# One byte offset for every slot of the matmuls' moving operand in a hybrid decoder layer

## The chip, the cores and the metric

The kernel runs on one core of a Trainium2 chip. The metric is the device time of one execution in microseconds (us); the median of three runs of the kernel before is 1404.62 us (1404.37 to 1404.83). A profile of one more execution says where the time goes.

## The reference

One inference step of a one-layer decoder trunk, in fp32, for 256 prompt tokens and 8 sample tokens of width 2048. Cut to the lines that matter:

```python
xn = rms_norm(x, g_mix)
z = xn @ w_in                                  # 2048 x 3584, split among three mixers
y_pool = pool_mixer(u_pool, ...) @ w_pool_br   # 512 -> 2048
y_lru = (h * gelu(u_gel)) @ w_lru_br           # 1024 -> 2048
y_conf = silu(layer_norm(vc, ...)) @ w_conf_br # 512 -> 2048
gates = sigmoid(xn @ w_gate + b_gate)          # 2048 -> 3 x 2048
x = x + (g_a * y_pool + g_b * y_lru + g_c * y_conf) @ w_out
hid = square(relu(rms_norm(x, g_mlp) @ w_up))  # 2048 -> 8192
x = x + hid @ w_down                           # 8192 -> 2048
```

A final RMSNorm follows, and the new states of the three mixers are outputs as well (the array `so_dram`).

## The kernel before

All tokens are worked on together: N = 256 + 8 = 264 columns. Activations lie transposed, 128 channels on the partitions and the 264 tokens along the free axis, so an operand with 2048 channels is 16 slots of 264 fp32 values, 1056 bytes in each partition. A slot is what one matmul streams as its moving operand.

To keep fp32 precision each operand is split into a high part (rounded to the type float32r) and a low part (the rest). One product is three matmuls, `mm3` (L193 to L196): high weights by high activations, high weights by low, low weights by high:

```python
nc.tensor.matmul(ps[:, :N], whi_t, xh, start=first, stop=False)    # L194
nc.tensor.matmul(ps[:, :N], whi_t, xl, start=False, stop=False)    # L195
nc.tensor.matmul(ps[:, :N], wlo_t, xh, start=False, stop=last)     # L196
```

**Operands.** `A` holds 32 slots: 0 to 15 high, 16 to 31 low. It is the operand of w_in, w_gate and w_out, and in the MLP the hidden layer of the first and the third quarter. The MLP's input lies in four tiles of eight slots, named xn2 (`M`, in `bpart`, L722 to L725; the profile writes "xn"), which take over the memory of the tiles `B`: two with the high parts, two with the low parts. The hidden layer of the second and fourth quarter is in `LH` (high) and `Q` (low); the LRU's gates use `L`, the branches `Q` and `LH`. In all of these slots lie one behind the other, 1056 bytes apart.

**Order of the work.** `weight_plan` lists groups, each one product with 512 output columns over up to 2048 input rows, and cuts them into 478 chunks of up to 128 x 1024 weights (two slots, `kt` 0 and 1, by 512 columns). The groups run: w_in (7 groups of 8 chunks; after four chunks of the lru groups the LRU's block weights come between), w_gate with w_pool_br and w_lru_br in four rounds, the last part of w_gate, w_conf_br, w_out, and then four quarters, each w_up (4 groups) and w_down (4 groups). For each slot the program issues four output tiles of three matmuls, twelve in all, before it goes on to the next slot; in the first four chunks (`by_operand`, L903) the same twelve are ordered by operand. The order is written out in Python, instruction by instruction; no scheduler moves it.

**Weights.** SyncE (SP) loads weights into a ring of six slots `raw`: `dma_pair` (L133 to L138) two chunks in one transfer of 1 MB from chunk SINGLE on, `dma_part` (L146) one chunk before. At chunk i the loads of chunks i + 8 and i + 9 are issued. ACT casts a chunk to its high part (`split`, L177) and DVE subtracts to get the low part (L178), three chunks ahead of TensorE (AHEAD = 3), into rings of four (`whi`, `wlo`). Between these casts ACT, DVE and GpSimd (POOL) do the mixers' elementwise work, handed out by costs and credits (`run_bg`).

**States.** The tile `st` collects the new states. At chunk 140 POOL issues its store to `so_dram` (L973).

**Memory.** In the built program the first 16384 bytes of each partition are scratch for transfers that POOL issues, then four constants of 32 bytes each, then the tiles in the order of their lines: raw, whi, wlo, qtmp (later Q), X, A, the four B tiles, L (later LH), G and small ones.

Of the kernel before, what the change touches and what calls it, by code (L numbers as in the profile page):

```python
# [9 lines left out]
F32 = mybir.dt.float32  # L10
F32R = mybir.dt.float32r
AF = mybir.ActivationFunctionType
ALU = mybir.AluOpType
AX = mybir.AxisListType

P = 128
D = 2048
TP = 256
TS = 8
N = TP + TS  # L20
KD = D // P
# [20 lines left out]
O_POOL, O_LC, O_CC, O_H = 1824, 1884, 1908, 2028  # L42
S_OUT = 2036

HEAD = N + 512
FIRST = 8
CH = 1024
# [2 lines left out]
LRU_AT = ((4, 1), (4, 3), (4, 5), (4, 6))  # L50
WARM = 17
LEAD = 4
SINGLE = 18
AHEAD = 3


# [31 lines left out]
def hybrid_step(ctx: ExitStack, tc: tile.TileContext, first, par_in, st_in, wall, y_out, st_out):  # L88
    nc = tc.nc
    cpool = ctx.enter_context(tc.tile_pool(name="cpool", bufs=1))  # L90
# [3 lines left out]
    def f(ap):  # L94
        return ap.bitcast(F32)
# [2 lines left out]
    raw = cpool.tile([P, NRAW, CH], F32, name="raw")  # L98
    whi = cpool.tile([P, NHI, CH], F32R, name="whi")
    wlo = cpool.tile([P, NHI, CH], F32R, name="wlo")  # L100
    qtmp = cpool.tile([P, 16 * N], F32, name="qtmp", tag="Q")
    X = cpool.tile([P, KD, N], F32, name="X")
    A = cpool.tile([P, 32, N], F32R, name="A")
    B = [cpool.tile([P, 8, N], F32, name=f"tmp{i}", tag=f"B{i}") for i in range(4)]
    L = cpool.tile([P, 16, N], F32R, name="L", tag="L")
    G = cpool.tile([P, 24, N], F32, name="G")
    par = cpool.tile([P, NPAR], F32, name="par")
    st = cpool.tile([P, S_OUT], F32, name="st")
# [7 lines left out]
    def pv(name, i=None, n=1):  # L116
        a, b = PCOL[name]
        return par[:, a:b] if i is None else par[:, a + i:a + i + n]

    def acc():  # L120
        return psum.tile([P, 512], F32, name="acc", tag="acc")

    spare = nc.const_aps.tensor(1.0, [P, 2 * P], dtype=mybir.dt.bfloat16)
    Gf = G.rearrange("p a n -> p (a n)")
    pext = qtmp[:, 2900:2900 + 4 * (15 + TP)].rearrange("p (g n) -> p g n", g=4)
    vext = B[3].rearrange("p a n -> p (a n)")[:, 8 * N - 4 * (30 + TP):].rearrange("p (g n) -> p g n", g=4)
    done = set()


# [16 lines left out]
        nc.sync.dma_start(raw[:, c % NRAW, a:b], src[:, a:b])  # L146


    head = [B[i].rearrange("p a n -> p (a n)") for i in (1, 2)]
    gm = head[0]  # L150

    def head_at(k):
# [136 lines left out]
    for c in range(2, 6):  # L289
        dma_x(c)  # L290
        dma_part(c, 0, CH)
    el = B[0].rearrange("p a n -> p (a n)")[:, :8 * (TP + 3)].rearrange("p (a n) -> p a n", a=8)
    nc.gpsimd.memset(el[:, :, 0:3], 0.0)
    nc.gpsimd.memset(vext[:, :, 0:30], 0.0)
    nc.gpsimd.memset(pext[:, :, 0:15], 0.0)
# [3 lines left out]
    def x_of(k):  # L299
        return head_x(k) if k < 4 else X[:, k, :]  # L300

    def x_high(k):
        if k < 2:
            nc.vector.tensor_scalar(A[:, k, :], x_of(k), gm[:, k:k + 1], None, op0=ALU.mult)
        else:
            nc.scalar.activation(A[:, k, :], x_of(k), AF.Copy, scale=gm[:, k:k + 1])

    def x_low(k):
        nc.vector.scalar_tensor_tensor(A[:, 16 + k, :], x_of(k), gm[:, k:k + 1], f(A[:, k, :]),
                                       op0=ALU.mult, op1=ALU.subtract)  # L310

    def x_tile(k):
# [407 lines left out]
    M = []  # L720

    def bpart(k):  # L722
        if not M:
            M.extend(cpool.tile([P, 8, N], F32R, name=f"xn2{i}", tag=f"B{i}") for i in range(4))
        return M[k // 8][:, k % 8, :], M[2 + k // 8][:, k % 8, :]  # L725

    def gate_tile(br, g, m):
        if br == 2:
# [8 lines left out]
    def gate_evac(br, g, m, ps):  # L737
        assert {"b_term", "grp"} <= done and (br != 1 or g % 2 == 0 or "lru" in done) and ("conf" in done or br < 2 or g < 3)
        t = gate_tile(br, g, m)
        nc.vector.tensor_tensor(t, ps[:, :N], rstd, op=ALU.mult)  # L740

        def rest():
            nc.scalar.activation(t, t, AF.Sigmoid, bias=pv("b_gate", br * 16 + g * 4 + m))
            spend(act=0.5)

        spend(dve=0.43)
        later(1 + m // 2, rest)

    def branch_evac(br, g, m, ps):
        assert "grp" in done and (br < 1 or "lru" in done) and (br < 2 or "conf" in done)  # L750
        t = gate_tile(br, g, m)
        k = g * 4 + m
        nc.vector.tensor_tensor(t, ps[:, :N], t, op=ALU.mult)
        spend(dve=0.43)
        if br == 1:
            nc.gpsimd.tensor_tensor(partial(k), t, gate_tile(0, g, m), op=ALU.add)
            spend(pool=0.8)
        if br == 2:
            nc.gpsimd.tensor_tensor(t, t, partial(k), op=ALU.add)
            spend(pool=0.8)  # L760
            later_split(A[:, k, :], A[:, 16 + k, :], t, 1)

    def later_split(hi, lo, x, n):
        def one():
            nc.scalar.copy(hi, x)
            spend(act=0.4)

        def other():
            nc.vector.tensor_tensor(lo, x, f(hi), op=ALU.subtract)
            spend(dve=0.35)  # L770

        later(n, one)
        later(n + 1, other)
# [31 lines left out]

    def hid(q, k):
        if q % 2 == 0:
            return A[:, k, :], A[:, 16 + k, :]
        return LH(k), Q(k)

    def up_evac(q, m, ps):
# [37 lines left out]
    def group(gi):  # L849
        name, k0, _, m = groups[gi]  # L850
        if name == "w_in":
            def rhs(i):
                return A[:, i, :], A[:, 16 + i, :]
            fn = {0: pool_evac, 1: lru_x_copy, 2: lambda c, p: lru_x_evac(4 + c, p), 3: gel_evac,
                  4: lambda c, p: gel_evac(4 + c, p), 5: ca_evac, 6: cb_evac}[m]
            return rhs, fn
        if name == "w_gate":
            return (lambda i: (A[:, i, :], A[:, 16 + i, :])), (lambda c, p: gate_evac(m // 4, m % 4, c, p))
        if name == "w_pool_br":
            assert "grp" in done  # L860
            return (lambda i: (Q(i), Q(8 + i))), (lambda c, p: branch_evac(0, m, c, p))
        if name == "w_lru_br":
            assert "lru" in done
            return (lambda i: (LH(i), LH(8 + i))), (lambda c, p: branch_evac(1, m, c, p))
        if name == "w_conf_br":
            assert "conf" in done
            return (lambda i: (Q(4 + i), Q(12 + i))), (lambda c, p: branch_evac(2, m, c, p))
        if name == "w_out":
            return (lambda i: (A[:, i, :], A[:, 16 + i, :])), (lambda c, p: out_evac(m * 4 + c, p))
        if name == "w_up":  # L870
            return bpart, (lambda c, p: up_evac(m // 4, (m % 4) * 4 + c, p))
        q = k0 // 16
        return (lambda i: hid(q, i)), (lambda c, p: down_evac(q, m * 4 + c, p))
# [52 lines left out]
    for i, ch in enumerate(chunks):  # L926
        now[0] = i
        if i < 5:
            x_tile(2 * i + 6)
            x_tile(2 * i + 7)  # L930
        for half in (0, 1) if i < 2 else (None,):
            split(i + AHEAD, half)
        if i == 12:
            softplus()
            again = first[:, KD:KD + 4 * HEAD].rearrange("p (k c) -> p k c", k=4)[:, :, :N]
            nc.sync.dma_start(X[:, 0:4, :], again)
            nc.vector.tensor_scalar(gfin, pv("g_final"), -0.5, None, op0=ALU.mult)
        if i % 2 == 0:
            dma_pair((i + 8) // 2)
        if i == 2:  # L940
            nc.sync.dma_start(par, par_in)
            nc.sync.dma_start(st[:, :S_IN], st_in)
        kind, gi, c, _ = ch
        if kind == "dense":
            rhs, fn = group(gi)
            n = groups[gi][2] // 2
            if c == 0:
                pss = [acc() for _ in range(4)]
            if i < len(chunks) - 2:
                for kt in range(2):  # L950
                    if i < LEAD:
                        by_operand(i, kt, rhs, pss)
                    for m in range(4 * (i < LEAD), 4):
                        tile_mm(i, c, kt, m, rhs, pss, c == n - 1 and kt == 1)
            elif i == len(chunks) - 1:
                for m in range(4):
                    for b in range(4):
                        tile_mm(i - 1 + b // 2, c - 1 + b // 2, b % 2, m, rhs, pss, b == 3)
            if c == n - 1:
                for m in range(4):  # L960
                    fn(m, pss[m])
                after(gi)
        elif kind == "lru":
            for j in range(2):
                lru_gate_mm(2 * gi + j, i, j)
            if gi == 3:
                lru_tail()
        elif kind == "grp":
            grp_mm(i)
        if i == len(chunks) - 4:  # L970
            nc.scalar.preload_act_table_set(ROOT)
        if i == 140:
            nc.gpsimd.dma_start(st_out, st)  # L973
        if 5 <= i < 9:
            x_squares(i - 5)
        if i == 9:
            later(0, x_sum)
        if i == 12:
            later(0, x_rms)
        run_bg()  # L980
# [9 lines left out]
    for h in range(2):  # L990
        for k, t in enumerate((20, 21 + (KD - 2) % 3, 11)):
            nc.tensor.matmul(ps[h][:, :H2], ones, G[:, t, half[h]], start=k == 0, stop=k == 2)  # L992
    out = [cpool.tile([P, KD, H2], F32, name=f"y{h}", tag=f"B{h}") for h in range(2)]
    last = [acc(), acc()]
    pool_r, tn = G[:, 10, :], G[:, 9, :]
    seed = [rstd[:, half[0]], acc()[:, :H2]]
# [128 lines left out]
```

## Time and profile before

| what | value |
|---|---|
| median of 3 runs | 1404.62 us |
| the profiled execution's own time | 1404.7 us |
| its span, first to last instruction | 1402.9 us |
| granted TensorE clock, mean | 0.998 |
| matmuls | 11421 |
| HBM traffic over the span | 182 GB/s |

The span is what the trace covers; about 1.8 us of the execution's time lie around it. In the profile's rows "PE" is TensorE, "PEld" its weight loads, which overlap the matmuls; matmuls overlap each other, so the duration of one is longer than the distance from one start to the next. A row of the timeline reads: start in us, duration in us, engine, line, operation, output <- inputs, shape. A row of a group ends with the busy time, the mean duration of one in ns, and the idle time before. "SPq" is SyncE's queue.

### The profile page before, as it was taken

To read this page: it belongs to the slowest core of one execution; us is meant where nothing else is said; L and a number is where in the kernel's file an instruction comes from. 1 tells how busy PE (TensorE), PEld (TensorE's weight loads), DVE (VectorE), ACT (ScalarE), POOL (GpSimd) and SP (SyncE) were. 2 spreads that over 40 slices of the span, in tenths; PEclk is the share of its full clock that TensorE was granted. 3 is DMA by queue.
4 is the path that set the end of the run, shared out by engine and by line. 5 is a ranking of instruction groups with operands and counts; after the bars stand their busy time and mean duration, and the time that the engine had idled before them with its cause. 6 is when DMAs were issued, how large, how long until landed. Compare 5 with 4: busy or idle time off the path is not lost.

```text
span 1402.9 us, 26642 instructions
## 1 busy us (share of the span) xinstructions
PE 1392.3 (99%) x11421; PEld 1390.5 (99%) x11421; DVE 835.8 (60%) x1052; ACT 722.3 (51%) x1021; POOL 94.3 (7%) x123
## 2 busy tenths in 40 slices
PE   9999999999999999999999999999999999999997
PEld 9999999999999999999999999999999999999997
DVE  8685787766766658565545444554455544455544
ACT  7757576656664645455544334543344533354544
POOL 0220010110102013010000000000000000000012
PEclk9999999999999999999999999999999999999999
DMA  9555555555655554555555555555555555555551
GB/s 363 170 173 188 185 185 191 181 182 181 210 182 180 179 182 160 202 177 172 192 181 181 180 182 180 181 180 182 179 182 178 183 179 182 181 181 179 180 183 74
DMA packets 39814, 257.49 MB, mean 184 GB/s; under 512 B 4368, under 2 KB 5520, under 8 KB 10896
## 3 DMA queue, kind: packets, MB, share of 16 engines
q1 hardware_dynamic: 39120, 254.15, 53.2%
q8 instruction: 89, 1.46, 0.4%
q0 software_dynamic: 144, 1.04, 0.2%
q10 hardware_dynamic: 432, 0.61, 0.1%
q14 instruction: 29, 0.24, 0.1%
HBM read 252.57 MB, written 3.21 MB: 182 GB/s over the span
## 4 chain that ended last, share of the span: by engine, by line
PE 99%; DVE 0%; DMA 0%; ACT 0%; DVEq 0%; issue 0%
PE acc L196 33%; PE acc L194 33%; PE acc L195 33%; PE acc L903 1%; DMA tmp<-first_dram 0%; DVE y L1014 0%; DVE acc L1005 0%; DVEq L1104 0%; DVE G L1004 0%; DVE acc L1003 0%; PE acc L992 0%; PE acc L271 0%; ACT whi L187 0%; ACT rstd L998 0%; DVE G L834 0%
## 5 line engine op out<-in xcount | busy, mean ns | idle before, releaser
L178 DVE TENSOR_TENSOR wlo<-raw,whi 128x1024 fp32r<-128x1024 f32 (+1 forms) x478 | 584.1, 1224 | 541.8 <-ACT whi L177 541.0
L177 ACT CAST whi<-raw 128x1024 fp32r<-128x1024 f32 (+1 forms) x478 | 495.3, 1039 | 614.2 <-PE acc L195 560.2
L194 PE MATMUL acc<-A,whi 128*128 128x264 f32 x1952 | 556.0, 285 | 0.0
L196 PE MATMUL acc<-A,wlo 128*128 128x264 f32 x1952 | 555.2, 284 | 0.0
L195 PE MATMUL acc<-A,whi 128*128 128x264 f32 x1952 | 554.3, 284 | 0.0
L195 PEld LDWEIGHTS acc<-A,whi 128*128 128x128 f32 x1952 | 368.8, 189 | 0.0
L196 PEld LDWEIGHTS acc<-A,wlo 128*128 128x128 f32 x1952 | 368.1, 189 | 0.0
L194 PEld LDWEIGHTS acc<-A,whi 128*128 128x128 f32 x1952 | 367.9, 188 | 0.0
L194 PE MATMUL acc<-xn,whi 128*128 128x264 f32 x1024 | 291.7, 285 | 0.0
L196 PE MATMUL acc<-xn,wlo 128*128 128x264 f32 x1024 | 291.3, 284 | 0.0
L195 PE MATMUL acc<-xn,whi 128*128 128x264 f32 x1024 | 290.8, 284 | 0.0
L195 PEld LDWEIGHTS acc<-xn,whi 128*128 128x128 f32 x1024 | 193.5, 189 | 0.0
L196 PEld LDWEIGHTS acc<-xn,wlo 128*128 128x128 f32 x1024 | 193.1, 189 | 0.0
L194 PEld LDWEIGHTS acc<-xn,whi 128*128 128x128 f32 x1024 | 193.0, 188 | 0.0
L195 PE MATMUL acc<-Q,whi 128*128 128x264 f32 x644 | 182.9, 284 | 0.0
L194 PE MATMUL acc<-LH,whi 128*128 128x264 f32 x640 | 182.3, 285 | 0.0
L196 PE MATMUL acc<-LH,wlo 128*128 128x264 f32 x640 | 182.0, 284 | 0.0
L195 PEld LDWEIGHTS acc<-Q,whi 128*128 128x128 f32 x644 | 121.7, 189 | 0.0
L196 PEld LDWEIGHTS acc<-LH,wlo 128*128 128x128 f32 x640 | 120.7, 189 | 0.0
L194 PEld LDWEIGHTS acc<-LH,whi 128*128 128x128 f32 x640 | 120.6, 188 | 0.0
L804 POOL TENSOR_TENSOR G<-G 128x264 f32<-128x264 f32 x28 | 25.7, 919 | 809.1 <-ACT G L802 808.2
L585 ACT ACTIVATE G<-tmp,par 128x256 f32<-128x256 f32 x120 | 54.3, 500 | 1.3 <-DVE G L599 0.7
(195 smaller groups left out, 792.5 us busy)
## 6 DMA issues: line engine op xcount, KB each, us to landing
raw<-wall_dram SPq DMA_DIRECT2D x225, 1024.0 KB, 4.9
raw<-wall_dram SPq DMA_DIRECT2D x14, 512.0 KB, 7.2
raw<-first_dram SPq DMA_DIRECT2D x6, 512.0 KB, 8.0
X<-first_dram SPq DMA_DIRECT2D x6, 264.0 KB, 7.8
raw<-wall_dram SPq DMA_DIRECT2D x5, 256.0 KB, 2.9
tmp<-first_dram SPq DMA_DIRECT2D x3, 388.0 KB, 5.1
so_dram<-st POOLq DMA_DIRECT2D x1, 1018.0 KB, 5.7
st<-st_dram SPq DMA_DIRECT2D x1, 912.0 KB, 8.8
```

Source lines behind the costliest of these rows:

```text
L177: nc.scalar.copy(h[:, s], r[:, s])
L178: nc.vector.tensor_tensor(lo[:, s], r[:, s], f(h[:, s]), op=ALU.subtract)
L194: nc.tensor.matmul(ps[:, :N], whi_t, xh, start=first, stop=False)
L195: nc.tensor.matmul(ps[:, :N], whi_t, xl, start=False, stop=False)
L196: nc.tensor.matmul(ps[:, :N], wlo_t, xh, start=False, stop=last)
L585: nc.scalar.activation(dst[:, ct, :TP], vext[:, ct, k:k + TP], AF.Copy, scale=par[:, w:w + 1])
L804: nc.gpsimd.tensor_tensor(sq2, sq2, t, op=ALU.add)
L903: nc.tensor.matmul(pss[m][:, :N], w[:, i % NHI, s], x, start=i == kt == k == 0, stop=False)
```

## The change

Each slot of A, and of the four tiles of the MLP's input, now starts PITCH = 320 values (1280 bytes) behind the one before, and the first SHIFT = 56 values (224 bytes) behind the start of its tile. So A grows from 33792 to 40960 bytes a partition and each B tile from 8448 to 10240. A and B move ahead of qtmp and X. The B tiles as scratch for the mixers keep their old layout: views on the first 8 x N values. To make room, the scratch for POOL's transfers shrinks from 16384 to 1024 bytes, and the store of the states, the one transfer that POOL issued, is issued by SyncE at the same chunk. SINGLE goes from 18 to 16: chunks 16 and 17 come in one transfer instead of two. In the built program the changed A starts at byte 58496 of each partition, the first B tile at 99456, Q at 140416 and L at 174208; before it was A 107648, B 141440, Q 73856 and L 175232.

```diff
+PITCH = 320
+SHIFT = 56
-SINGLE = 18
+SINGLE = 16
...
+    a_all = cpool.tile([P, SHIFT + 31 * PITCH + N], F32R, name="A")
+    b_all = [cpool.tile([P, SHIFT + 7 * PITCH + N], F32, name=f"tmp{i}", tag=f"B{i}") for i in range(4)]
     qtmp = cpool.tile([P, 16 * N], F32, name="qtmp", tag="Q")
     X = cpool.tile([P, KD, N], F32, name="X")
-    A = cpool.tile([P, 32, N], F32R, name="A")
-    B = [cpool.tile([P, 8, N], F32, name=f"tmp{i}", tag=f"B{i}") for i in range(4)]
+    B = [b[:, :8 * N].rearrange("p (a n) -> p a n", a=8) for b in b_all]
...
+    def operand(t, k):
+        at = SHIFT + k * PITCH
+        return t[:, at:at + N]
+
+    def A(k):
+        return operand(a_all, k)
...
     def bpart(k):
         if not M:
-            M.extend(cpool.tile([P, 8, N], F32R, name=f"xn2{i}", tag=f"B{i}") for i in range(4))
-        return M[k // 8][:, k % 8, :], M[2 + k // 8][:, k % 8, :]
+            M.extend(cpool.tile([P, SHIFT + 7 * PITCH + N], F32R, name=f"xn2{i}", tag=f"B{i}") for i in range(4))
+        return operand(M[k // 8], k % 8), operand(M[2 + k // 8], k % 8)
...
         if i == 140:
-            nc.gpsimd.dma_start(st_out, st)
+            nc.sync.dma_start(st_out, st)
...
-    nc = _bacc.Bacc("TRN2", target_bir_lowering=False, num_devices=1)
+    nc = _bacc.Bacc("TRN2", target_bir_lowering=False, num_devices=1, dynamic_dma_scratch_size=1024)
```

Every use of `A[:, k, :]` becomes `A(k)`, and the views on whole B tiles (`head`, `el`, `vext`, the output tiles) are cut from `b_all`.

More of the change, by code (lines that the diff above doesn't have):

```diff
@@ L125, in hybrid_step @@
     pext = qtmp[:, 2900:2900 + 4 * (15 + TP)].rearrange("p (g n) -> p g n", g=4)
-    vext = B[3].rearrange("p a n -> p (a n)")[:, 8 * N - 4 * (30 + TP):].rearrange("p (g n) -> p g n", g=4)
+    vext = b_all[3][:, 8 * N - 4 * (30 + TP):8 * N].rearrange("p (g n) -> p g n", g=4)
     done = set()
@@ L146, in dma_part @@
         nc.sync.dma_start(raw[:, c % NRAW, a:b], src[:, a:b])
-    head = [B[i].rearrange("p a n -> p (a n)") for i in (1, 2)]
+    head = [b_all[i] for i in (1, 2)]
     gm = head[0]
@@ L291, in hybrid_step @@
         dma_part(c, 0, CH)
-    el = B[0].rearrange("p a n -> p (a n)")[:, :8 * (TP + 3)].rearrange("p (a n) -> p a n", a=8)
+    el = b_all[0][:, :8 * (TP + 3)].rearrange("p (a n) -> p a n", a=8)
     nc.gpsimd.memset(el[:, :, 0:3], 0.0)
@@ L303, in x_high @@
         if k < 2:
-            nc.vector.tensor_scalar(A[:, k, :], x_of(k), gm[:, k:k + 1], None, op0=ALU.mult)
+            nc.vector.tensor_scalar(A(k), x_of(k), gm[:, k:k + 1], None, op0=ALU.mult)
         else:
-            nc.scalar.activation(A[:, k, :], x_of(k), AF.Copy, scale=gm[:, k:k + 1])
+            nc.scalar.activation(A(k), x_of(k), AF.Copy, scale=gm[:, k:k + 1])
     def x_low(k):
-        nc.vector.scalar_tensor_tensor(A[:, 16 + k, :], x_of(k), gm[:, k:k + 1], f(A[:, k, :]),
+        nc.vector.scalar_tensor_tensor(A(16 + k), x_of(k), gm[:, k:k + 1], f(A(k)),
                                        op0=ALU.mult, op1=ALU.subtract)
@@ L760, in branch_evac @@
             spend(pool=0.8)
-            later_split(A[:, k, :], A[:, 16 + k, :], t, 1)
+            later_split(A(k), A(16 + k), t, 1)
     def later_split(hi, lo, x, n):
@@ L807, in hid @@
         if q % 2 == 0:
-            return A[:, k, :], A[:, 16 + k, :]
+            return A(k), A(16 + k)
         return LH(k), Q(k)
@@ L852, in rhs @@
             def rhs(i):
-                return A[:, i, :], A[:, 16 + i, :]
+                return A(i), A(16 + i)
             fn = {0: pool_evac, 1: lru_x_copy, 2: lambda c, p: lru_x_evac(4 + c, p), 3: gel_evac,
@@ L857, in group @@
         if name == "w_gate":
-            return (lambda i: (A[:, i, :], A[:, 16 + i, :])), (lambda c, p: gate_evac(m // 4, m % 4, c, p))
+            return (lambda i: (A(i), A(16 + i))), (lambda c, p: gate_evac(m // 4, m % 4, c, p))
         if name == "w_pool_br":
@@ L868, in group @@
         if name == "w_out":
-            return (lambda i: (A[:, i, :], A[:, 16 + i, :])), (lambda c, p: out_evac(m * 4 + c, p))
+            return (lambda i: (A(i), A(16 + i))), (lambda c, p: out_evac(m * 4 + c, p))
         if name == "w_up":
@@ L992, in hybrid_step @@
             nc.tensor.matmul(ps[h][:, :H2], ones, G[:, t, half[h]], start=k == 0, stop=k == 2)
-    out = [cpool.tile([P, KD, H2], F32, name=f"y{h}", tag=f"B{h}") for h in range(2)]
+    out = [cpool.tile([P, SHIFT + 7 * PITCH + N], F32, name=f"y{h}", tag=f"B{h}")[:, :KD * H2]
+           .rearrange("p (k n) -> p k n", k=KD) for h in range(2)]
     last = [acc(), acc()]
```

## The prediction

> **What bounds the kernel now.** I read the page first, part 1 and then the chain of part 4.
>
> ```profile
> span 1402.9 us, 26642 instructions
> PE 1392.3 (99%) x11421; PEld 1390.5 (99%) x11421; DVE 835.8 (60%) x1052; ACT 722.3 (51%) x1021; POOL 94.3 (7%) x123
> PEclk9999999999999999999999999999999999999999
> PE 99%; DVE 0%; DMA 0%; ACT 0%; DVEq 0%; issue 0%
> ```
>
> The chain that ended last is TensorE's own stream for 99% of the span, at a full granted clock: no transfer and no other engine sets the end. So the time is the number of matmuls times the interval from the start of one to the start of the next, and little else. The reader must not take the "mean ns of one" for that interval: matmuls overlap, so the rows below say 284 ns each while a new one starts every 0.12 us. Their counts are what I use.
>
> ```profile
> L194 PE MATMUL acc<-A,whi 128*128 128x264 f32 x1952 | 556.0, 285 | 0.0
> L196 PE MATMUL acc<-A,wlo 128*128 128x264 f32 x1952 | 555.2, 284 | 0.0
> L195 PE MATMUL acc<-A,whi 128*128 128x264 f32 x1952 | 554.3, 284 | 0.0
> L194 PE MATMUL acc<-xn,whi 128*128 128x264 f32 x1024 | 291.7, 285 | 0.0
> L196 PE MATMUL acc<-xn,wlo 128*128 128x264 f32 x1024 | 291.3, 284 | 0.0
> L195 PE MATMUL acc<-xn,whi 128*128 128x264 f32 x1024 | 290.8, 284 | 0.0
> ```
>
> ```profile
> 4.77 12.04 PE acc L903 x96
> ```
>
> The last row is the chain's: the 96 matmuls of the first four chunks, on A as well. Matmuls whose moving operand lies in A: 3 x 1952 + 96 = 5952. In the MLP's input (tiles xn2, "xn" in the rows): 3 x 1024 = 3072. Together 9024 of 11421; the others stream L, LH and Q, which the change leaves as they are.
>
> Next the timeline of TensorE alone, where consecutive rows give the interval. For each slot k of an operand the program issues twelve matmuls (four output tiles, three each), all streaming slot k. A slot is 264 x 4 = 1056 bytes, which is 32 modulo 256, so the byte at which the stream starts, modulo 256, goes round in eight slots. In the built program A lies at byte 107648 of each partition, and the four xn2 tiles from 141440 on: both 128 modulo 256, so slots 0 to 7 start at 128, 160, 192, 224, 0, 32, 64, 96. The high and the low half of a slot lie a multiple of 256 apart and share that byte. These rows are the first matmul of slots 0 to 7 and of the next slot, in the second quarter of w_up, with the third matmul of slots 1, 4 and 7:
>
> ```profile
> 830.52 0.28 PE L194 MATMUL acc<-xn,whi 128*128 128x264 f32 x1
> ...
> 831.98 0.29 PE L194 MATMUL acc<-xn,whi 128*128 128x264 f32 x1
> ...
> 832.23 0.28 PE L196 MATMUL acc<-xn,wlo 128*128 128x264 f32 x1
> ...
> 833.44 0.29 PE L194 MATMUL acc<-xn,whi 128*128 128x264 f32 x1
> ...
> 834.89 0.28 PE L194 MATMUL acc<-xn,whi 128*128 128x264 f32 x1
> ...
> 836.34 0.29 PE L194 MATMUL acc<-xn,whi 128*128 128x264 f32 x1
> ...
> 836.60 0.29 PE L196 MATMUL acc<-xn,wlo 128*128 128x264 f32 x1
> ...
> 837.83 0.29 PE L194 MATMUL acc<-xn,whi 128*128 128x264 f32 x1
> ...
> 839.29 0.28 PE L194 MATMUL acc<-xn,whi 128*128 128x264 f32 x1
> ...
> 840.76 0.29 PE L194 MATMUL acc<-xn,whi 128*128 128x264 f32 x1
> ...
> 841.00 0.28 PE L196 MATMUL acc<-xn,wlo 128*128 128x264 f32 x1
> ...
> 842.20 0.28 PE L194 MATMUL acc<-xn,whi 128*128 128x264 f32 x1
> ```
>
> Twelve matmuls of one slot take 1.46, 1.46, 1.45, 1.45, 1.49, 1.46, 1.47 and 1.44 us in turn. Byte 0 is the slowest, byte 96 the fastest, and nothing else differs between these rows: same line, shape, clock and no wait. Inside a slot the first two intervals still carry the step from the byte before; from the third matmul on, ten intervals take 833.44 - 832.23 = 1.21 us at byte 160, 1.23 at byte 0, and 842.20 - 841.00 = 1.20 at byte 96. So a run at byte 96 goes at 120.0 ns a matmul.
>
> The mean over whole stretches comes from the start of w_up's second quarter above and these two rows, the start of w_down's first quarter (A) and the end of w_up's second:
>
> ```profile
> 737.02 0.28 PE L194 MATMUL acc<-A,whi 128*128 128x264 f32 x1
> ```
>
> ```profile
> 924.01 0.28 PE L194 MATMUL acc<-LH,whi 128*128 128x264 f32 x1
> ```
>
> A: 830.52 - 737.02 = 93.50 us for 64 slots x 12 = 768 matmuls, 121.74 ns. xn2: 924.01 - 830.52 = 93.49 us, 121.73 ns. The two operands behave alike.
>
> **The change part by part.** *The pitch.* In the changed program A starts at byte 58496 and the four B tiles at 99456 and every 10240 after: all 128 modulo 256. SHIFT adds 224 bytes and PITCH steps by 1280 = 5 x 256, so every slot of A and xn2 streams from byte 96. Every matmul, weight load and cast stays, in the same order; only addresses move. L, LH, Q and the weight tiles keep their bytes modulo 256. The gain is 9024 x (121.73 - 120.0) ns = 15.6 us, all of it on the chain. The same by slots: 752 x (1460.8 - 1440) ns = 15.6.
>
> The 120.0 needs one more support, as no row shows two slots running at one byte. This is a slot of A at byte 0, entered from L at byte 160 instead of from byte 224 as usual:
>
> ```profile
> 105.91 0.28 PE L194 MATMUL acc<-A,whi 128*128 128x264 f32 x1
> ...
> 106.15 0.28 PE L196 MATMUL acc<-A,wlo 128*128 128x264 f32 x1
> ...
> 107.35 0.28 PE L194 MATMUL acc<-A,whi 128*128 128x264 f32 x1
> ```
>
> It takes 1.44 us, 0.24 for the first two and 1.20 for ten. So 120 ns looks like the floor of this shape at any byte, and what comes on top depends on the byte and on how it was entered. I take the floor for all 9024, neither less (no long run of rows shows less) nor, as bound on the other side, the 1.445 us that a slot at byte 96 takes now with its entry (1.44 by the rows, which round).
>
> Now a rule that speaks against the change. The Trainium skill, "TensorE: Matmul & The Clock Gate", section "Step-by-step: what each phase is for", says that throughput is purely N cycles, one column a cycle, and its section "Back-to-back issue gap" gives N / 2.4 + 2.5 ns: an estimate of 112.5 ns for 264 columns wherever the operand lies. By it the sum would be 0. The trace disagrees with it on both counts: 121.7 ns, and between 1.44 and 1.49 us for twelve equal matmuls.
>
> *The store of the states* moves from POOL's queue to SP's, between two weight loads.
>
> ```profile
> SPq L138 <- DVE wlo L178: 1205.0, 223, 9.6
> ```
>
> ```profile
> L518 POOL COPY st<-tmp x1: 193/193/193, 189.8 to 189.8; 128x8 f32<-128x8 f32 x1
> ```
>
> ```profile
> 400.29 17.87 SPq L138 DMA_DIRECT2D raw<-wall_dram  x4
> ```
>
> ```profile
> raw<-wall_dram SPq DMA_DIRECT2D x225, 1024.0 KB, 4.9
> so_dram<-st POOLq DMA_DIRECT2D x1, 1018.0 KB, 5.7
> ```
>
> The state tile's last writer ends by 190 us, and SP reaches chunk 140's loads after 400, so the store waits for nothing; and SP, which in all waits 1205 us for casts to free weight slots, is not a queue that runs late. Behind it in SP's queue is the next pair of weight chunks. Loads issue about every 5.9 us (17.87 over three gaps). A load is issued when its slot is free and cast some four chunks later (24 matmuls each, 2.92 us): 11.7 us, against 4.9 + 5.7 = 10.6 if the two go strictly one after the other. Cost 0. Without that cover a cast would be up to 5.7 us late, and casts run three chunks (8.8 us) ahead of TensorE, so it still would not reach it.
>
> *SINGLE 16* makes one load of chunks 16 and 17, which waits for both slots.
>
> ```profile
> 20.63 11.20 SPq L146 DMA_DIRECT2D raw<-wall_dram  x6
> ```
>
> ```profile
> 44.11 1.04 ACT L177 CAST whi<-raw 128x1024 fp32r<-128x1024 f32 x1
> ```
>
> The six are chunks 12 to 17; the last is issued by 31.83 us. The cast at 44.11 is chunk 16's. It lands 4.9 us after its issue by the median above, or 8.8 if it fares like the slowest of the large early loads, the states':
>
> ```profile
> st<-st_dram SPq DMA_DIRECT2D x1, 912.0 KB, 8.8
> ```
>
> That is 40.6 at the latest, 3.5 us ahead of the cast. Cost 0.
>
> *Scratch of 1 KB* only makes room: the store was the last transfer issued by POOL. Cost 0; I allow 0.5 us either way for these three edits and the shifted start.
>
> *What is late next.* With TensorE 1.4% faster in these stretches, ACT and DVE must cast 1.4% faster.
>
> ```profile
> 150.00:200.00 50.00, 50.00 (x413) 50.00 (x412) 41.99 (x59) 28.13 (x39) 5.91 (x6) 1.00 0.51 170
> ```
>
> ```profile
> ACT whi L177 <- PE acc L195: 560.2, 351, 3.7
> ```
>
> Among eight stretches of the first 450 us the DVE is fullest here: 41.99 of 50 us, in which 1.4% more makes 42.6. ACT's casts wait 560 us in all for TensorE to free a buffer: the casts are ahead, not behind.
>
> Sum: -15.6 and 0. The profiled execution took 1404.7 us, the median shown is 1404.62, so 1404.7 - 15.6 = **1389.1 us**, and the same for the median.
>
> **The rivals.**
>
> *The entry cost stays* (0.09). If the extra in the first two matmuls of a slot comes from the change of weight rows and not of byte, a slot keeps 1445 ns: gain 752 x 15.8 = 11.9 us, 1392.8. Against: slot 4 in the last timeline has no such extra, though its weights changed as well.
>
> *Bad entries* (0.05). The slot at byte 0 shows that a pattern depends on how it was entered. w_in (7 x 16 slots, cold start and four interruptions by L) and the 40 slots of w_gate after the pool's matmuls enter byte 96 in ways that no row shows, and an even byte no longer shakes a bad pattern off. At byte 0's 123 ns these 152 slots lose 152 x 12 x 3 = 5.5 us: 1394.6. The other 600 enter from byte 96 as they leave LH and Q at slot 7 or 15.
>
> *Address does not matter* (0.03): the interval follows something else that goes round with k, and the time stays 1404.6. For: four weight buffers of two halves go round in eight, too. Against it stand two rows of w_in, the first matmuls of A's slots 4 and 5 in chunk 10, which lies in weight buffer 2 (10 modulo 4), while the slot at byte 0 of the first timeline is chunk 288's, in buffer 0:
>
> ```profile
> 34.16 0.29 PE L194 MATMUL acc<-A,whi 128*128 128x264 f32 x1
> ...
> 35.65 0.29 PE L194 MATMUL acc<-A,whi 128*128 128x264 f32 x1
> ```
>
> 1.49 us again: the slow slot goes with the byte and not with the weight buffer. The Trainium skill's rule on N cycles, above, would end in this rival.
>
> *Slower* (0.03): one byte for all turns out a fixed bad pattern, and the changing byte was what shook it off. The place is the 9024 matmuls; the price at byte 0's 123 ns is 9024 x 1.27 = 11.5 us, 1416.2; it decides from 121.73 ns on. For: byte 0 holds its 123 for ten matmuls without recovering. Against: byte 96 holds 120.
>
> *It doesn't do what it says*: excluded, since the built addresses give byte 96 everywhere.
>
> **How the numbers follow.** Forecast 1389.1 with 0.80, entry cost 1392.8 with 0.09, bad entries 1394.6 with 0.05, no effect 1404.6 with 0.03, slower 1416.2 with 0.03. The range takes the forecast and the entry cost with 0.5 us for the side edits and some for the runs' own scatter: 1387.8 to 1393.3. A measurement of this kernel tells about 0.2% (2.8 us) from no change: faster 0.94, same 0.03, slower 0.03.
>
> **What would show it.** In the timeline of the changed kernel every slot of A and xn2 takes 1.44 us, a quarter of w_up 64 x 1.44 = 92.16 us instead of 93.49, and w_down's second and fourth quarters still 93.5. The entry cost would show as 0.245 us at the first two of a slot; bad entries as w_in longer than 1.44 a slot while w_up has it; the store as a load near 412 us landing late and an ACT cast that waits for a DMA. The forecast is wrong if the quarters of w_up keep 93.5, or if TensorE gets idle times with a cast as releaser.

## The result and the profile after

The changed kernel takes 1389.34 us (median of 4 runs, 1388.89 to 1389.54) against 1404.72 us of the kernel before (1404.37 to 1405.1): ratio 0.989, interval 0.9874 to 0.9905. That is 15.4 us less. The profiled execution took 1389.49 us. Its page:

```profile
span 1387.7 us, 26639 instructions
PE 1377.4 (99%) x11421; PEld 1375.6 (99%) x11421; DVE 836.2 (60%) x1052; ACT 722.1 (52%) x1021; POOL 93.5 (7%) x122
PE 99%; DVE 0%; DVEq 0%; ACT 0%; issue 0%
```

The chain is TensorE's stream as before, with the same 11421 matmuls; the span is 15.2 us shorter. The timeline of TensorE, at the start of w_up's second quarter (slot 0, its third matmul, slots 1 and 2), at the end of that quarter, and at the end of w_down's second quarter:

```profile
820.74 0.28 PE L204 MATMUL acc<-xn,whi 128*128 128x264 f32 x1
...
820.98 0.28 PE L206 MATMUL acc<-xn,wlo 128*128 128x264 f32 x1
...
822.18 0.28 PE L204 MATMUL acc<-xn,whi 128*128 128x264 f32 x1
...
823.62 0.28 PE L204 MATMUL acc<-xn,whi 128*128 128x264 f32 x1
```

```profile
912.90 0.28 PE L204 MATMUL acc<-LH,whi 128*128 128x264 f32 x1
```

```profile
1006.38 0.28 PE L204 MATMUL acc<-xn,whi 128*128 128x264 f32 x1
```

Every slot takes 1.44 us, its first two intervals 0.24. The quarter of w_up takes 92.16 us where it took 93.49; the quarter of w_down that streams LH and Q still takes 1006.38 - 912.90 = 93.48. The gain lies where the slots moved; the quarter whose slots stayed gains nothing.

What was watched beside it. The casts:

```profile
ACT whi L187 <- PE acc L205: 549.2, 350, 3.7
```

```profile
150.00:200.00 50.00, 50.00 (x419) 50.00 (x418) 42.51 (x60) 29.80 (x42) 5.87 (x6) 1.00 0.50 173
```

ACT still waits for TensorE, 11 us less in all; the DVE's fullest stretch went from 41.99 to 42.51 us of 50, 1.2% more where 1.4% was expected. The double load of chunks 16 and 17 (the first of these two issues), and chunk 16's cast:

```profile
31.58 6.15 SPq L148 DMA_DIRECT2D raw<-wall_dram  x2
```

```profile
43.95 1.04 ACT L187 CAST whi<-raw 128x1024 fp32r<-128x1024 f32 x1
```

It was issued at 31.58 us, where the prediction had 31.83, and the cast, at 44.11 before, is on time. The store of the states from SP's queue, its issue and that of the next loads:

```profile
so_dram<-st SPq DMA_DIRECT2D x1, 1018.0 KB, 9.4
```

```profile
402.14 0.42 SPq L983 DMA_DIRECT2D so_dram<-st  x1
407.52 17.72 SPq L148 DMA_DIRECT2D raw<-wall_dram  x4
```

It took 9.4 us to land, where POOL's took 5.7. The cover that the prediction computed (11.7 us against two transfers in series) would not have held with 9.4 + 4.9 = 14.3. But the two ran partly side by side: the next load was issued 5.4 us behind the store, while the store was still under way, and no load between 395 and 430 us took more than 7.4 us to land. No cast between 395 and 450 us waits for a transfer, so the store cost nothing.

### The profile page after: what moved, and what is told of

It is laid out like the page before. It is cut to its first block, busy times and chain, and to the rows that moved or that the text cites. A ratio compares the mean times of both kernels' runs of the same rounds, so it can differ in the third digit from the quotient of the medians.

```text
span 1387.7 us, 26639 instructions
## 1 busy us (share of the span) xinstructions
PE 1377.4 (99%) x11421; PEld 1375.6 (99%) x11421; DVE 836.2 (60%) x1052; ACT 722.1 (52%) x1021; POOL 93.5 (7%) x122
## 4 chain that ended last, share of the span: by engine, by line
PE 99%; DVE 0%; DVEq 0%; ACT 0%; issue 0%
PE acc L204 33%; PE acc L205 33%; PE acc L206 32%; PE acc L913 1%; PE acc L298 0%; DVE y L1025 0%; DVE acc L1016 0%; DVEq L1115 0%; DVE G L1015 0%; DVE acc L1014 0%; PE acc L1002 0%; PE acc L281 0%; ACT rstd L1009 0%; DVE G L844 0%; DVE X L843 0%
## 5 line engine op out<-in xcount | busy, mean ns | idle before, releaser
L205 PE MATMUL acc<-A,whi 128*128 128x264 f32 x1952 | 551.2, 282 | 0.0
L206 PE MATMUL acc<-A,wlo 128*128 128x264 f32 x1952 | 548.6, 281 | 0.0
L205 PEld LDWEIGHTS acc<-A,whi 128*128 128x128 f32 x1952 | 365.9, 187 | 0.0
L205 PE MATMUL acc<-xn,whi 128*128 128x264 f32 x1024 | 288.9, 282 | 0.0
L206 PE MATMUL acc<-xn,wlo 128*128 128x264 f32 x1024 | 287.2, 281 | 0.0
L205 PEld LDWEIGHTS acc<-xn,whi 128*128 128x128 f32 x1024 | 192.0, 188 | 0.0
L205 PE MATMUL acc<-Q,whi 128*128 128x264 f32 x644 | 182.9, 284 | 0.0
L205 PEld LDWEIGHTS acc<-Q,whi 128*128 128x128 f32 x644 | 121.7, 189 | 0.0
```

## Experiments

Two questions were open. Is byte 96 special, or does any one byte for all slots give the floor of 120 ns, as the prediction supposed from the slot at byte 0 that took 1.44 us? And what is the floor? Every kernel differs from the changed kernel in the lines shown, unless the text says the kernel before; but for sides, wbyte0 and both128, tiles keep their places and sizes, so that no other address moves. Times beside a ratio are medians of timed runs; the others are one run with its profile, whose differences are read from the trace. The rows quoted are the starts of w_up's second quarter and of the group after it: 64 slots.

**sides.** The kernel before with the side edits alone.

```diff
-SINGLE = 18
+SINGLE = 16
...
-            nc.gpsimd.dma_start(st_out, st)
+            nc.sync.dma_start(st_out, st)
...
-    nc = _bacc.Bacc("TRN2", target_bir_lowering=False, num_devices=1)
+    nc = _bacc.Bacc("TRN2", target_bir_lowering=False, num_devices=1, dynamic_dma_scratch_size=1024)
```

> The kernel before with the three side edits alone: SINGLE 16, the states' store from SyncE, 1 KB of scratch; the slots stay 1056 bytes apart. Theory (the side edits only make room and cost nothing): 1404.7 us, within 0.5. Rival (a part of the gain is theirs, by the store's other queue or the earlier double load): below 1403 us.

Measured 1404.64 us, ratio 1.0 (0.9991 to 1.0009).

```profile
830.49 0.28 PE L194 MATMUL acc<-xn,whi 128*128 128x264 f32 x1
```

```profile
923.98 0.28 PE L194 MATMUL acc<-LH,whi 128*128 128x264 f32 x1
```

93.49 us, as before. The side edits gain and cost nothing, although they move every tile by 15360 bytes: a multiple of 256.

**a_only.** A at byte 96, the MLP's input as before.

```diff
-        return operand(M[k // 8], k % 8), operand(M[2 + k // 8], k % 8)
+        at = k % 8 * N
+        return M[k // 8][:, at:at + N], M[2 + k // 8][:, at:at + N]
```

> The changed kernel with only A at byte 96; the MLP's input has its slots 1056 bytes apart again. Theory (the parts add up by their matmuls): w_up's four quarters go back to 93.49 us each, 4 x 1.33 = 5.3 us more than the changed kernel, 1394.6 us. Rival (the gain needs unbroken runs at one byte, so that w_down and w_out lose too where w_up stands next to them): above 1396 us.

Measured 1395.0 us. The start of w_down's first quarter (A), w_up's second (xn2) and the next:

```profile
730.09 0.28 PE L204 MATMUL acc<-A,whi 128*128 128x264 f32 x1
```

```profile
822.25 0.28 PE L204 MATMUL acc<-xn,whi 128*128 128x264 f32 x1
```

```profile
915.74 0.28 PE L204 MATMUL acc<-LH,whi 128*128 128x264 f32 x1
```

A takes 92.16 us and xn2 93.49 beside it. The parts add up: four quarters of w_up are worth 5.3 us, and the run is 5.7 above the changed kernel.

**byte0.** All slots at byte 0.

```diff
-        at = SHIFT + k * PITCH
+        at = 32 + k * PITCH
```

> The changed kernel with every slot of A and of the MLP's input at byte 0 modulo 256 instead of 96, same pitch, same tiles. Theory (one byte for all slots gives the floor, whichever byte): 1440 ns a slot as at byte 96, so 1389.3 us. Rival (byte 96 is a good byte, and byte 0 a bad one): 123 ns a matmul, as ten intervals at byte 0 took 1.23 us before, so 9024 x 3.0 ns = 27 us more than the changed kernel, 1416 us, slower than the kernel before.

Measured 1415.04 us, ratio 1.0072 (1.0057 to 1.0087): slower than the kernel before, as the rival said.

```profile
836.15 0.29 PE L204 MATMUL acc<-xn,whi 128*128 128x264 f32 x1
```

```profile
930.87 0.29 PE L204 MATMUL acc<-LH,whi 128*128 128x264 f32 x1
```

94.72 us for 64 slots, 1480 ns each, 123.3 a matmul. But not everywhere. Two stretches of w_gate in the same run, all on A at byte 0, the first entered from the pool's matmuls, the second from LH (each pair is its first matmul and the first one behind it):

```profile
189.84 0.28 PE L204 MATMUL acc<-A,whi 128*128 128x264 f32 x1
```

```profile
247.43 0.29 PE L204 MATMUL acc<-Q,whi 128*128 128x264 f32 x1
```

```profile
306.07 0.28 PE L204 MATMUL acc<-A,whi 128*128 128x264 f32 x1
```

```profile
353.43 0.29 PE L204 MATMUL acc<-Q,whi 128*128 128x264 f32 x1
```

The first runs 40 slots in 57.59 us, 1440 ns each; the second 32 slots in 47.36 us, 1480 each. So byte 0 has two steady rates, and which one a stretch keeps changes with how it is entered. The slot that the prediction quoted had been entered the good way. "Any one byte" falls.

**byte128.** All slots at byte 128.

```diff
-        at = SHIFT + k * PITCH
+        at = 0 + k * PITCH
```

> The changed kernel with every slot of A and of the MLP's input at byte 128 modulo 256. Theory (any one byte gives the floor): 1389.3 us. Rival (each byte has a rate of its own): byte 128 took 1.46 us a slot and some 121.3 to 121.6 ns a matmul behind its entry, so 12 to 14 us more, 1401 to 1404 us.

Measured 1398.39 us, ratio 0.9954 (0.994 to 0.9969).

```profile
825.15 0.28 PE L204 MATMUL acc<-xn,whi 128*128 128x264 f32 x1
```

```profile
918.34 0.28 PE L204 MATMUL acc<-LH,whi 128*128 128x264 f32 x1
```

93.19 us, 1456 ns a slot in the MLP: neither reading as it stood. The total is below the rival's 1401 because part of the early stages ran at the floor, as these 42 slots of w_in and w_gate, 60.49 us:

```profile
123.57 0.28 PE L204 MATMUL acc<-A,whi 128*128 128x264 f32 x1
```

```profile
184.06 0.28 PE L204 MATMUL acc<-Q,whi 128*128 128x264 f32 x1
```

**byte64 and byte224.** The same line with 48 and with 24 in place of SHIFT.

> Every slot of A and of the MLP's input at byte 64 modulo 256. Theory (each byte has one or two steady patterns; the floor is 1440 ns a slot, and whether a byte leaves it depends on the byte): before, byte 64 needed 1466 ns a slot, but the intervals that follow its entry went up to 131 ns and came back to 120, so at one byte it should settle on the floor: 1389.3 us. Rival (the mean of a byte before is its rate): 1466 - 1440 = 26 ns a slot, 19.6 us more, 1409 us.

> Every slot of A and of the MLP's input at byte 224 modulo 256. Before, its twelve intervals (118 to 129 ns, 1455 ns a slot) show no period, so the two readings stand as: floor reached, 1389.3 us; a rate of its own as the slot before had, 1455 - 1440 = 15 ns a slot, 11.3 us more, 1400.6 us. The theory that only the floor or a pattern above it occurs says one of the two for long stretches, not a mean between them.

Measured 1389.65 us at byte 64 and 1408.04 at byte 224. The rows of byte 64, then of byte 224:

```profile
820.84 0.28 PE L204 MATMUL acc<-xn,whi 128*128 128x264 f32 x1
```

```profile
913.00 0.29 PE L204 MATMUL acc<-LH,whi 128*128 128x264 f32 x1
```

```profile
834.17 0.28 PE L204 MATMUL acc<-xn,whi 128*128 128x264 f32 x1
```

```profile
927.61 0.28 PE L204 MATMUL acc<-LH,whi 128*128 128x264 f32 x1
```

Byte 64 is on the floor, 92.16 us, although it was one of the slow bytes before (1.47 us a slot): there the byte changed from slot to slot, here it does not. Byte 224 goes at 93.44 us, 1460 ns a slot, and never reaches the floor. Its early stages are slower still in part, as these 42 slots of w_in, 63.83 us or 1520 ns a slot:

```profile
44.42 0.28 PE L204 MATMUL acc<-A,whi 128*128 128x264 f32 x1
```

```profile
108.25 0.28 PE L204 MATMUL acc<-L,whi 128*128 128x264 f32 x1
```

The total is therefore above both expected times. Pitch and place of the tiles are those of the changed kernel in these four runs, from byte0 to byte224, so neither gives the gain by itself. The expectation "one of the two" missed: 1460 is neither 1440 nor the slot's 1455 of before.

**pitch1088.** Slots 1088 bytes apart, at bytes 96, 160, 224 and 32 in turn.

```diff
-        at = SHIFT + k * PITCH
+        at = SHIFT + k * 272
```

> The changed kernel with slots of A and of the MLP's input 1088 bytes apart, so that they start at bytes 96, 160, 224, 32 modulo 256 in turn, all 32 modulo 64. If what must not change is the byte modulo 64 or less: 1389.3 us. If it is the byte modulo 256 (theory, since the pattern before goes round in eight slots of 32 bytes): the mean of the four slots as measured before, 1445, 1458, 1455 and 1465 ns, 1455.7, so 752 x 15.7 ns = 11.8 us more, about 1401 us, with other entries perhaps 1393 to 1405.

Measured 1406.88 us, ratio 1.0014 (1.0005 to 1.0024).

```profile
832.64 0.29 PE L204 MATMUL acc<-xn,whi 128*128 128x264 f32 x1
```

```profile
926.28 0.29 PE L204 MATMUL acc<-LH,whi 128*128 128x264 f32 x1
```

93.64 us, a little more than before, and above the range of 1393 to 1405 that was expected: the mean of the four bytes' old slots did not carry over. The byte modulo 64 is not enough, and a shorter round of bytes gains nothing.

**third256 and third128.** What is the floor? The third product of each triple, over 256 and over 128 columns; the low weights' part is left out for the other 8 and 136 tokens:

```diff
-        nc.tensor.matmul(ps[:, :N], wlo_t, xh, start=False, stop=last)
+        nc.tensor.matmul(ps[:, :TP], wlo_t, xh[:, :TP], start=False, stop=last)
```

```diff
-        nc.tensor.matmul(ps[:, :N], wlo_t, xh, start=False, stop=last)
+        nc.tensor.matmul(ps[:, :P], wlo_t, xh[:, :P], start=False, stop=last)
```

> The changed kernel with the third product of each triple (low weights) over 256 of the 264 columns, outside the first four chunks: the low weights' part for the 8 sample tokens is left out. It asks what the floor of 120.0 ns is. If it is the columns at one each 1/2.4 ns and a fixed 24 cycles: the third goes at 116.7 ns, 3764 x 3.33 = 12.5 us less, 1376.8 us. If it is the weight load ahead of each matmul, or anything that does not shrink with the columns: 1389.3 us, unchanged, with other patterns at 96 at most some us above.

> The changed kernel with the third product of each triple (low weights) over only 128 of the 264 columns, outside the first four chunks: the low weights' part for half of the prompt and the 8 sample tokens is left out. At 256 columns the floor did not move, which speaks for the weight load or another cost that does not shrink with the columns. If so, also here 120 ns a matmul: 1388 to 1390 us. If the columns do count beyond some point (3764 matmuls with 136 columns, 57 ns, less), down to 1389 - 213 = 1176 us.

Measured 1388.93 us and 1371.77 us: 8 columns less change nothing in the total that can be told, and 136 less in every third matmul only 17.6 us of the 213. w_up's second quarter takes 92.40 us with 256 columns (from 821.29 to 913.69) and 91.30 with 128 (from 811.52 to 902.82), against 92.16 with all. So 8 columns less gain nothing at the floor. They do gain in the quarter behind it, which streams LH and Q at changing bytes (92.48 us instead of 93.48); the total hides both. TensorE's matmuls, and then its weight loads, in w_up with 128 columns:

```profile
812.05 0.28 PE L205 MATMUL acc<-xn,whi 128*128 128x264 f32 x1
812.17 0.22 PE L206 MATMUL acc<-xn,wlo 128*128 128x128 f32 x1
812.23 0.34 PE L204 MATMUL acc<-xn,whi 128*128 128x264 f32 x1
812.41 0.28 PE L205 MATMUL acc<-xn,whi 128*128 128x264 f32 x1
```

```profile
812.05 0.19 PEld L206 LDWEIGHTS acc<-xn,wlo 128*128 128x128 f32 x1
812.17 0.19 PEld L204 LDWEIGHTS acc<-xn,whi 128*128 128x128 f32 x1
812.28 0.19 PEld L205 LDWEIGHTS acc<-xn,whi 128*128 128x128 f32 x1
812.41 0.19 PEld L206 LDWEIGHTS acc<-xn,wlo 128*128 128x128 f32 x1
```

The short matmul does let the next one start after 0.06 us, but the one behind that starts only 0.18 us later: from one L205 to the next it is 0.36 us, as with full columns. The weight loads stay 0.11 to 0.13 us apart. So it is not the columns that set the floor. The rows fit weight loads that set it; no run changed a weight load's size, so that is not shown. It made one more question: if TensorE reads weights all the time, does their byte count?

**wbyte0.** Both weight rings 128 bytes further on, from byte 128 to byte 0; the tiles behind them move by 256 bytes, so the operands stay at byte 96.

```diff
-    whi = cpool.tile([P, NHI, CH], F32R, name="whi")
-    wlo = cpool.tile([P, NHI, CH], F32R, name="wlo")
+    whi = cpool.tile([P, 32 + NHI * CH], F32R, name="whi")[:, 32:].rearrange("p (a c) -> p a c", a=NHI)
+    wlo = cpool.tile([P, NHI * CH + 32], F32R, name="wlo")[:, :NHI * CH].rearrange("p (a c) -> p a c", a=NHI)
```

> The changed kernel with the weight rings whi and wlo 128 bytes further on: weights start at byte 0 modulo 256 instead of 128, the operands stay at byte 96. If only the operand's own byte counts: 1440 ns a slot, 1389.3 us. If the distance between weights and operand counts (the rival: 96 is good because weights are read from 128 on at the same time), byte 96 now stands as byte 224 did and gives 1460 to 1520 ns a slot: 1404 to 1410 us.

Measured 1420.1 us, the slowest of all and above the 1404 to 1410 that the rival gave.

```profile
842.21 0.29 PE L204 MATMUL acc<-xn,whi 128*128 128x264 f32 x1
```

```profile
939.49 0.28 PE L204 MATMUL acc<-LH,whi 128*128 128x264 f32 x1
```

97.28 us, 1520 ns a slot, with the operand at the byte that gave 1440. The operand's own byte does not decide. Nor is 1520 this kernel's only rate: w_down's third quarter, on A at the same byte, takes 93.44 us, 1460 ns a slot:

```profile
1126.43 0.28 PE L204 MATMUL acc<-A,whi 128*128 128x264 f32 x1
```

```profile
1219.87 0.28 PE L204 MATMUL acc<-xn,whi 128*128 128x264 f32 x1
```

These are the two rates that byte 224 had with the weights at byte 128.

**both128.** The same, and the operands 128 bytes further on as well, to byte 224.

```diff
-        at = SHIFT + k * PITCH
+        at = 24 + k * PITCH
```

> The kernel of the run before (weights 128 bytes further on, at byte 0) with the operands moved by 128 bytes as well, to byte 224: the distance from weights to operand is that of the changed kernel, the operand's own byte is the one that gave 1408 us. If the distance modulo 256 decides: 1440 ns a slot, 1389.3 us. If the operand's byte has a part of its own, or 0 is a bad byte for the weights whatever the operand does: 1460 ns a slot or more, 1404 to 1420 us.

Measured 1388.8 us.

```profile
820.13 0.28 PE L204 MATMUL acc<-xn,whi 128*128 128x264 f32 x1
```

```profile
912.29 0.29 PE L204 MATMUL acc<-LH,whi 128*128 128x264 f32 x1
```

92.16 us: the floor, at the byte that took 1408.04 us with the weights at 128. So what counts is the operand's byte minus the weights', modulo 256. Two distances were run with the weights at both places: 224 gave the floor at both, and 96 gave the same pair of rates at both. The other three were run with the weights at one place only:

| distance | kernels | ns a slot |
|---|---|---|
| 224 | changed kernel, both128 | 1440 |
| 192 | byte64 | 1440 |
| 0 | byte128 | 1456, in part 1440 |
| 128 | byte0 | 1480, in part 1440 |
| 96 | byte224, wbyte0 | 1460, in part 1520, in each of the two |

**hid_a.** A version beyond both kernels: the hidden layer of every quarter in A, at distance 224, since w_down's reads of A end before the next w_up writes it.

```diff
     def hid(q, k):
-        if q % 2 == 0:
-            return A(k), A(16 + k)
-        return LH(k), Q(k)
+        return A(k), A(16 + k)
```

> The changed kernel, and the hidden layer of all four quarters in A (byte 96) instead of LH and Q in the second and fourth. Theory (what streams from byte 96 runs at 1440 ns a slot): w_down's second and fourth quarters take 92.16 instead of 93.49 us each, 128 slots x 20.8 ns = 2.7 us less than the changed kernel, 1386.7 us. Rival (A as the only buffer makes the casts of the next quarter wait for w_down's last reads, and the next w_down for the casts): TensorE idle at the three quarter borders, some 1 to 3 us each, 1390 to 1396 us.

Measured 1386.44 us (1386.41 to 1386.63), ratio 0.987 (0.9853 to 0.9886) to the kernel before.

```profile
820.35 0.28 PE L204 MATMUL acc<-xn,whi 128*128 128x264 f32 x1
```

```profile
912.51 0.28 PE L204 MATMUL acc<-A,whi 128*128 128x264 f32 x1
```

```profile
1004.67 0.28 PE L204 MATMUL acc<-xn,whi 128*128 128x264 f32 x1
```

w_up and w_down both take 92.16 us now, and TensorE waits for nothing at the border.

## Why the prediction was right

*The gain, 9024 x 1.73 ns = 15.6 us, 1389.1.* Measured 15.4 and 1389.34. Every stretch of groups on A and xn2 runs at 1440 ns a slot, but for the start and a few slots behind an entry.

*The side edits, 0 within 0.5 us.* The kernel sides took 1404.64 us, against 1404.68 of the kernel before beside it.

*The entry cost, the first rival.* Gone: 0.24 us for the first two matmuls of a slot where the distance stays the same.

*The support for 120.0: "the floor of this shape at any byte".* This step was wrong, though the number was right. byte0 holds 1480 and byte224 1460 ns a slot for hundreds of microseconds. The forecast held because the rows of byte 96 themselves had shown 120.0 for ten matmuls, and because byte 96 comes back to the floor from every entry that this kernel has. That much was luck: a slot's time in the kernel before does not tell the steady rate of its byte. Byte 64 took 1.47 us there and runs at 1440 ns, byte 224 took 1.45 and runs at 1460 or 1520. And the prediction had only the operand's byte; the weights' byte, on which the choice of 96 depends as much, is no term of it.

*"Bad entries" and "slower".* Both mechanisms exist, at other bytes: at byte 0 the rate depends on the entry, and one fixed bad byte cost 10.4 us there, against the 11.5 that the prediction gave for it. It was right to ask for them and right to put them low for byte 96.

*"Address does not matter".* Refuted by byte0 and wbyte0. Its argument, though, that the weight buffers go with it was nearer than its price: the weights' place counts, by their byte and not by their buffer, and all buffers of this kernel lie at the same byte. The Trainium skill's formula N / 2.4 + 2.5 ns, which the prediction set against the change, stands in "TensorE: Matmul & The Clock Gate", section "Back-to-back issue gap", as the gap of a matmul standing alone, not of a stream of weight loads and matmuls. So the 112.5 ns worked out from it was no figure for this kernel, whose 11421 matmuls come with 11421 weight loads, and no run here tests the formula.

*The store, "10.6 if the two go strictly one after the other".* The term was too small: the store took 9.4 us, not POOL's 5.7. Its cost was still 0, as it ran beside the loads and no cast came late.

## What to carry to other kernels

Where matmuls bound a kernel and each comes with a weight load, compare the distance of their starts, not their durations, slot by slot: a pattern that goes round with the slot index points at addresses. Give the moving operand's slots one distance to the weights modulo 256 and choose it by trial (here 224 or 192; 0, 96 and 128 cost up to 80 ns in twelve matmuls, and 32, 64 and 160 were not tried by themselves), checking that it holds from every entry. A pad for that can be paid with memory that nothing needs, as here the scratch, or not be needed at all where one buffer can serve twice (hid_a).

## What the runs showed of the hardware that was not expected

The time of a stream depends on the bytes of weights and moving operand together: the same operand at byte 96 takes 1440 ns a slot with weights at byte 128, and 1460 or 1520 with weights at byte 0. The Trainium skill, "TensorE: Matmul & The Clock Gate", section "Step-by-step: what each phase is for", says that loading the next tile's weights does not steal read bandwidth from the running matmul, since the two have ports of their own. By that the weights' place would not show; moving the weights alone took 1389.34 us to 1420.1, and moving the operands along brought it back to 1388.8. What in the chip the two share no run shows. The section "Back-to-back issue gap" of that page of the Trainium skill says that in a stream of weight loads and matmuls both set the spacing; third128 agrees: three matmuls still take some 0.36 us when the third of them is cut to half.

The rate can have two steady values at one distance, and a stretch keeps the one that it entered with: 1440 and 1480 ns a slot at distance 128 (byte0, 57.59 us at the floor), 1460 and 1520 at distance 96 (wbyte0). Why there are two stays open. The step of 256 bytes fits too: distances 128 apart differ (224 and 96, 0 and 128), while successive slots, 1280 = 5 x 256 bytes apart, do not.

And the start: the first eight matmuls of the changed kernel's profiled run took 0.7 us longer than those of the kernel before, which these rows show (changed, then before; the second column is the time of the group):

```profile
4.48 1.97 PE L913 MATMUL acc<-A,whi 128*128 128x264 f32 x8
```

```profile
4.77 1.26 PE L903 MATMUL acc<-A,whi 128*128 128x264 f32 x8 [0.21 <-ACT whi L187]
```

Less the 0.29 us by which the stream started earlier, that is the 0.4 us by which the span missed the forecast gain, 15.2 against 15.6 us. It goes with the granted clock. The trace's record of the full granted clock starts at 6.16 us of the span in the changed kernel and at 4.43 us, ahead of these matmuls, in the kernel before; until it starts the matmuls follow one another every 0.22 us instead of 0.12. Over the 14 kernels of this case that record starts between 3.43 and 6.59 us, and the first twelve matmuls take between 1.57 and 2.41 us, longest where it starts late. One execution of each was profiled, so no edit is shown to move it.
